# Two feed-forward stages of a hybrid transformer on Trainium2: weight splits issued earlier in the first, squares summed in two halves and a held first product in the second

## The chip, the cores and the metric

The kernel runs on one core of one Trainium2 chip, as one program. The metric is the device time of one execution in microseconds; lower is better. The core's engines work at the same time, each through its own instruction stream in a fixed order: TensorE (PE, matmuls; its weight loads are listed as PEld), VectorE (DVE), ScalarE (ACT), GpSimd (POOL). SyncE (SP) issues the DMAs.

## The reference

Two layers over 512 latent tokens and 256 context tokens of width 1024, in float32. Layer 0 mixes by grouped attention, layer 1 by a gated recurrence (HGRN2) in both directions; each is followed by a gated feed-forward (SwiGLU, hidden width 2816). Norms are modulated by vectors made from a condition `c`. Cut to what matters here:

```python
h = h + gt1_l * y_l                      # y_l: attention or recurrence, after its output product w_o
h = h + gt2_l * swiglu(modulate(rms_norm(h, norm_ffn_w[i]), sh2_l, sc2_l), ffn_w_in[i], ffn_w_out[i])

def rms_norm(x, w):                      # sum of squares over the 1024 features of a token
    return x * lax.rsqrt(jnp.mean(x * x, axis=-1, keepdims=True) + NORM_EPS) * w

def swiglu(h, w_in, w_out):
    a, u = jnp.split(h @ w_in, 2, axis=-1)
    return (jax.nn.silu(a) * u) @ w_out
```

The first feed-forward (layer 0) works on 768 tokens (latent and context), the second on 512.

## The kernel before

Activations are kept transposed: `hT[o]` holds 128 features (row o of 8) by all tokens. Every float32 product is made as three matmuls of a faster format (`mm3`, lines 114 to 118): each operand is split into a high part and a low part, hi x hi, hi x lo, lo x hi. `split` makes them: the high part is a cast on ACT (L88), the low part a subtraction on DVE or POOL (L93). Weights arrive by DMA in a ring of four raw buffers, `load_next` (L922) queues the next one on SP when an older buffer has been split.

A feed-forward (`ffn`) takes the hidden width in 22 units of 128 columns, each with two weight blocks, `("w", j, 0)` for a and `("w", j, 1)` for u. In the text w01 is block 1 of unit 0, and so on. The first units (two in layer 0, four in layer 1) are computed plainly: `plain_split` splits a unit's weights, `plain` multiplies them with the tokens in two halves of H columns, `plain_hidden` makes silu(a) * u and splits it into `gh` and `gl`. All later units use Strassen's scheme (Winograd's form) of seven products per unit, `m1` to `m7`, on the four quarters b11, b12, b21, b22 of the normalised input `x`. It needs sums of weight quarters, made on POOL in place in the raw buffers (`sums`, L1147 to L1150, and `sum4`, L1155), and differences of input quarters (t1 to t4). Each weight operand is one entry of a list of units, split in list order by `split_next`. The first entry's quarter a11 is overwritten by `sums`, so `sums` follows its split; the second entry, a12, is followed by `sum4`.

The start of each feed-forward overlaps with the end of the mixer before it:

- Layer 0, `start_attention`: the plain units run while POOL and DVE form the differences (L1294 and L1298 on POOL, L1301 and L1305 on DVE). Behind the last differences come two calls of `split_next`. Then PE goes on with `m1`, `m2`, `m5` (its bank is y), `m6` (operand t2), `m4` (bank w, operand t4).
- Layer 1, `start_recurrence`: `hgrn_wo_last` yields the recurrence's output rows in two halves of 256 tokens, eight rows each. A row is a few matmuls into a bank `hwo` and a residual addition on DVE (L687). Rows 6 and 7 of a half share a bank. For each row ACT squares it (L275, the first directly into the accumulator, L271) and POOL adds the square to `acc_n` (L276). Then `rstd_cols` sums over the features with matmuls against ones (`ssq`, L282), DVE and POOL make the reciprocal root (`rc`, L289 and L291), `rstd_psum` spreads it over partitions (DVE L297, PE L301), and `xhalf` makes the normalised and modulated operand of one row: DVE L960, ACT L962, cast L88, low part L93. Then come the first products (`ffi`).

A planner orders each engine's instructions before the kernel runs. It starts from program order and moves an instruction ahead when its own model of the times says that it is ready earlier. `pin` ties an instruction behind the one that the program issues just before it on the same engine. In `split`, `late="h"` pins the cast and `late="l"` the subtraction.

Of the kernel before, what the change touches and what calls it, by code (L numbers as in the profile page):

```python
# [8 lines left out]
F32 = mybir.dt.float32  # L9
# [7 lines left out]
P = 128  # L17
D = 1024
KT = D // P
# [28 lines left out]
def kernel(  # L48
# [10 lines left out]
    PE, DVE, ACT, POOL = nc.tensor, nc.vector, nc.scalar, nc.gpsimd  # L59
# [20 lines left out]
    def bank(name):  # L80
        return psums["pool"].tile([P, 512], F32, tag="b", bufs=psums["bufs"]["b"], name=name)
# [29 lines left out]
        split(hi, lo, raw, eng, hi_eng)  # L111
        return hi, lo

    def mm3(ps, ahi, alo, bhi, blo, first, last, onto=False):
        kw = dict(skip_group_check=True) if onto else {}
        PE.matmul(ps, ahi, bhi, start=first, stop=False, **kw)  # L116
        PE.matmul(ps, ahi, blo, start=False, stop=False, **kw)  # L117
        PE.matmul(ps, alo, bhi, start=False, stop=last, **kw)  # L118

    pin = tc.keep_in_program_order  # L120
# [34 lines left out]
    ones = cst.tile([P, P], F32, name="ones")  # L155
# [119 lines left out]
            ACT.activation(sq, h, AF.Square)  # L275
            (eng or DVE).tensor_tensor(acc, acc, sq, op=ALU.add)  # L276

    def rstd_cols(pl, acc, n, tag="rc", late=False):
        nt = n // P
        pc = bank("ssq")  # L280
        for t in range(nt):
            m = PE.matmul(pc[:, 2 * t : 2 * t + 2], acc[:, t * P : (t + 1) * P], ones[:, 0:2], start=True, stop=True)  # L282
            if late:
                pin(m)
        return rstd_of(pl, pc, nt, tag)

    def rstd_of(pl, pc, nt, tag="rc"):
# [586 lines left out]
    def ffn(layer, only_lat, pre, begin, tail=None):  # L874
        n = NL if only_lat else T
        H = n // 2
# [24 lines left out]
        def ctile(tag, bufs):  # L901
            return fp.tile([P, H], F32, tag=tag, bufs=bufs, name=tag)
# [40 lines left out]
        def plain_split(j, i, late=""):  # L943
            if j > 1 or i == 0 and (j == 0 or not layer):
                t = ring_tile()
            else:
                slot, p_ = {(0, 1): (3, fp), (1, 0): (1, fp), (1, 1): (2, fp if layer else hnp)}[j, i]
                t = [p_.tile([P, 4 * H], F32R, tag=f"xt{slot}{c}", name=f"w{j}1{c}")[:, 0:1024] for c in "hl"]
            pool_ = (j, i) == (0, 0) or j > 1 and i if layer else j == 0
            split(t[0], t[1], raws.pop(("w", j, i)), POOL if pool_ else DVE, late=late)  # L950
            w0[j, i] = t

# [10 lines left out]
            xh, xl = xops[("b1" if k < 4 else "b2") + "12"[h]]  # L963
            split(xh[:, k % 4], xl[:, k % 4], x[k][:, a0:e0], DVE if k % 2 else POOL)

        def plain(ps, j, i, k, h, first, last):
            hi, lo = w0[j, i]
            xh, xl = xops[("b1" if k < 4 else "b2") + "12"[h]]
            c = slice(k * P, (k + 1) * P)
            if h not in ps:  # L970
                ps[h] = xbank("ffi")[:, 0:H]
            mm3(ps[h], hi[:, c], lo[:, c], xh[:, k % 4], xl[:, k % 4], first, last)

        gh, gl = {}, {}

# [6 lines left out]
        def plain_hidden(j, h, psa, psu):  # L982
            c = ctile("c22", 2)
            ACT.activation(c, psa[h], AF.Silu)
            DVE.tensor_tensor(c, psu[h], c, op=ALU.mult)
            split(gh[j][:, h * H : h * H + H], gl[j][:, h * H : h * H + H], c)
# [254 lines left out]
        def start_attention():  # L1241
# [54 lines left out]
            for i in range(4):  # L1296
                b11, b12, b21, b22 = blocks(i)
                pin(POOL.tensor_tensor(b12, b22, b12, op=ALU.subtract))  # L1298
            for i in range(4):
                b11, b12, b21, b22 = blocks(i)  # L1300
                pin(DVE.scalar_tensor_tensor(b22, b11, -1.0, b22, op0=ALU.mult, op1=ALU.subtract))  # L1301
            plain_hidden(0, 1, *ps0)
            for i in range(4):
                b11, b12, b21, b22 = blocks(i)
                pin(DVE.scalar_tensor_tensor(b21, b22, -1.0, b21, op0=ALU.mult, op1=ALU.subtract))  # L1305
            split_next()
            split_next()
            xops["t3"] = operand("t3")
            for i in range(4):
                xsplit("t3", i, x[i][:, H:n])  # L1310
# [9 lines left out]
        def start_recurrence():  # L1320
# [4 lines left out]

            def products(j, h, i, ks):
                for k in ks:
                    plain(ps[j][i], j, i, k, h, k == 0, k == KT - 1)

            for h in range(2):  # L1330
                hs = slice(h * H, (h + 1) * H)
                for i in range(KT):
                    o = next(pre)
                    sumsq_add(acc_n[:, hs], fp, hT[o][:, hs], o, i == 0, POOL, tag="sw", bufs=2, width=512)
                    if h == 0 and i == 0:
                        plain_split(0, 0, "l")
                    if h == 0 and i == KT - 1:
                        plain_split(0, 1, "l")
                    if h == 1 and i == 1:
                        plain_split(1, 0, "l")  # L1340
                    if h == 1 and i == 2:
                        rst[0] = rstd_psum(ctile("c22", 2), rc[0], H)
                    if h == 1 and i >= 4:
                        xhalf(i - 4, 0)
                rc[h] = rstd_cols(fp, acc_n[:, hs], H, f"rc{h}")
            for _ in pre:
                pass
            for _ in range(2):
# [1 line left out]
            for k in range(KT):  # L1350
                if k >= 4:
                    xhalf(k, 0)
                for i in range(2):
                    products(0, 0, i, [k])
            plain_split(1, 1, "l")
            rst[1] = rstd_psum(ctile("c22", 2), rc[1], H)
            for k in order[:2]:
                xhalf(k, 1)
# [8 lines left out]
            for i_, k in enumerate(order):  # L1367
                for i in range(2):
                    plain(ps[0][i], 0, i, k, 1, i_ == 0, i_ == KT - 1)
            plain_split(2, 0)  # L1370
            plain_split(2, 1, "l")
            for _ in range(2):
                load_next()
# [374 lines left out]
    def hgrn_wo_last():  # L1748
        ks = (GH - 2, GH - 1)
        wo = []  # L1750
        for k in ks:
            t = [ring.tile([P, 1024], F32R, tag=tag, bufs=3, name=f"{tag}_hwo{k}") for tag in ("whi", "wlo")]
            split(t[0], t[1], hv.pop(("w", k)))
            wo.append(t)
        banks = []

        def first_rows(h):
            oh, ol = hv["o", GH - 2]
            a, e = h * (NL // 2), (h + 1) * (NL // 2)
            for o in range(6):  # L1760
                osl = slice(o * P, (o + 1) * P)
                if h == 0:
                    banks.append(xbank("hwo"))
                mm3(banks[o][:, a:e], wo[0][0][:, osl], wo[0][1][:, osl], oh[:, a:e], ol[:, a:e], True, False, True)

        first_rows(0)
        yield None
        os_ = [hv.pop(("o", k)) for k in ks]
        for h, (_, a, e) in enumerate(SPH):
            both = bank("hwo") if h == 0 else None  # L1770
            for o in range(KT):
                osl = slice(o * P, (o + 1) * P)
                if o < 6:
                    ps, todo = banks[o][:, a:e], (1,) if h == 0 else (0, 1)
                else:
                    both = both or xbank("hwo")
                    ps, todo = both[:, (o - 6) * 256 : (o - 6) * 256 + 256], (0, 1)
                for i in todo:
                    mm3(ps, wo[i][0][:, osl], wo[i][1][:, osl], os_[i][0][:, a:e], os_[i][1][:, a:e],
                        i == 0, i == 1, True)  # L1780
                residual(o, ps, 1, 2, 0, a, e)
                yield o

# [116 lines left out]
```

## Time and profile before

| | |
|---|---|
| runs | 1820.36, 1823.32, 1823.44 us; median 1823.32 |
| profiled execution | 1821.68 us, span of its instructions 1819.9 us |
| granted TensorE clock, mean | 0.99 |
| matmuls | 11749, PE busy 1755.3 us |
| first feed-forward's start | about 455 to 505 us of the span |
| second feed-forward's start | about 1437 to 1515 us of the span |
| HBM read | 162.36 MB, 90 GB/s |

Times in rows are microseconds from the span's start, and a row of one engine in order of time begins with its start and its length; neighbours of the same form are merged (xN), and square brackets give idle time of the engine before the row and what ended it. A waits row reads: who waited, for whom, microseconds in total, times, the longest. A windows row gives each engine's busy microseconds, with the number of instructions, in one stretch. Matmuls are pipelined: one may start before the last has ended, so the pace is read from starts or from counts.

### The profile page before, as it was taken

How to read it: one execution, taken by the hardware profiler on the slowest of the kernel's cores; microseconds unless marked ns; L12 is line 12 of the kernel's file. 1: busy time of each engine (PE TensorE's matmuls, PEld its weight loads, DVE VectorE, ACT ScalarE, POOL GpSimd, SP SyncE). 2: the span in 40 equal slices, each digit the busy share in tenths (PEclk: the TensorE clock that was granted, in tenths of full speed). 3: DMA queues.
4: the chain of work that ended last, by engine and by line, in shares of the span. 5: the costliest groups of instructions: out<-in, count | busy, mean ns of one | idle time of the engine just before them, and what ended most of it. 6: DMA issues, size and time to landing. Idle time of an engine off the chain costs nothing.

```text
span 1819.9 us, 30696 instructions
## 1 busy us (share of the span) xinstructions
PE 1755.3 (96%) x11749; PEld 1606.9 (88%) x11749; DVE 1300.5 (71%) x2291; ACT 867.2 (48%) x1768; POOL 637.7 (35%) x583
## 2 busy tenths in 40 slices
PE   8988999999999999999999999999999899999998
PEld 6778678988899999999998999899898799999997
DVE  4587588888888878787865555665747758786764
ACT  4342787676642424333354443343434445554545
POOL 1244254345522304131414333144325544443420
PEclk9999999999999999999999999999999999999999
DMA  8533520002124243445331211222211223333322
GB/s 319 176 105 84 163 79 24 1 24 64 30 87 129 73 137 93 146 133 153 108 116 34 70 59 59 70 82 70 81 56 38 67 59 112 101 106 106 99 60 83
DMA packets 213459, 166.45 MB, mean 91 GB/s; under 512 B 7952, under 2 KB 190400, under 8 KB 213312
## 3 DMA queue, kind: packets, MB, share of 16 engines
q1 hardware_dynamic: 213024, 163.43, 29.2%
q8 instruction: 93, 1.52, 0.4%
q10 hardware_dynamic: 288, 1.05, 0.1%
q14 instruction: 54, 0.44, 0.1%
HBM read 162.36 MB, written 2.10 MB: 90 GB/s over the span
## 4 chain that ended last, share of the span: by engine, by line
PE 78%; DVE 9%; POOL 4%; ACT 4%; issue 2%; DMA 2%; SPq 0%; POOLq 0%; DVEq 0%; ACTq 0%
PE ffo L118 5%; PE ffo L116 5%; PE ffo L117 5%; PE x L116 4%; PE x L117 4%; PE x L118 4%; PE pt L714 3%; PE y L118 2%; PE y L116 2%; PE y L117 2%; PE lv L1643 2%; PE hz L116 2%; PE hz L117 2%; PE hz L118 2%; PE sc L656 2%
## 5 line engine op out<-in xcount | busy, mean ns | idle before, releaser
L1650 POOL TENSOR_TENSOR KD<-KD,tot 128x384 f32<-128x384 f32 x96 | 102.6, 1092 | 82.1 <-ACT kc L1633 78.4
L704 POOL TENSOR_SCALAR pf<-pf,st 128x768 f32<-128x768 f32 (+1 forms) x96 | 73.6, 769 | 128.1 <-DVE st L703 91.6
L687 DVE SCALAR_TENSOR_TENSOR hT<-ffo,modc,hT 128x512 f32<-128x512 f32 (+1 forms) x122 | 78.7, 649 | 48.2 <-PE ffo L118 48.2
L118 PE MATMUL ffo<-gh,wlo_w 128*128 128x512 f32 (+1 forms) x304 | 102.9, 339 | 0.0
L117 PE MATMUL ffo<-gl,whi_w 128*128 128x512 f32 (+1 forms) x304 | 102.4, 337 | 0.0
L116 PE MATMUL ffo<-gh,whi_w 128*128 128x512 f32 (+1 forms) x304 | 102.0, 338 | 0.0
L239 DVE SCALAR_TENSOR_TENSOR adacc<-adw,csil,adacc 128x512 f32<-128x512 f32 x98 | 84.5, 871 | 7.5 <-DMA adw<-in_ada_w_dram 7.4
L93 DVE TENSOR_TENSOR ptl<-pt,pth 128x384 fp32r<-128x384 f32 (+1 forms) x160 | 79.9, 524 | 12.4 <-ACT pth L88 11.2
L88 ACT CAST pth<-pt 128x384 fp32r<-128x384 f32 (+1 forms) x160 | 69.9, 461 | 34.3 <-PE pt L714 22.6
L700 DVE TENSOR_REDUCE st<-sc 128x1 f32<-128x768 f32 (+1 forms) x96 | 74.2, 773 | 15.3 <-PE sc L657 12.6
L702 ACT ACTIVATE pf<-sc,st 128x768 f32<-128x768 f32 (+1 forms) x96 | 73.4, 765 | 19.3 <-DVE st L700 18.4
L1650 DVE TENSOR_TENSOR QD<-QD,tot 128x256 f32<-128x256 f32 x96 | 52.0, 582 | 41.2 <-PE lv L1643 41.1
L1633 ACT COPY kc<-KD 128x256 f32<-128x256 f32 x112 | 43.4, 414 | 75.8 <-PE lv L1643 43.8
L714 PE MATMUL pt<-ident,pf 128*128 128x128 f32 x448 | 72.2, 275 | 5.2 <-DVE ptl L93 3.9
L116 PE MATMUL ffo<-gh,foh 128*128 128x512 f32 (+1 forms) x186 | 71.4, 384 | 0.0
L118 PE MATMUL ffo<-gh,fol 128*128 128x512 f32 (+1 forms) x186 | 70.8, 381 | 0.2 <-DVE fol L93 0.2
L117 PE MATMUL ffo<-gl,foh 128*128 128x512 f32 (+1 forms) x186 | 70.9, 381 | 0.0
L1709 POOL TENSOR_SCALAR oss<-oss 128x4 f32<-128x4 f32 (+1 forms) x9 | 4.7, 524 | 181.8 <-DVE oss L1708 181.7
L1643 PE MATMUL lv<-QD,kc 128*128 128x128 f32 x448 | 63.4, 286 | 4.5 <-DVE QD L1650 2.4
L1643 PEld LDWEIGHTS lv<-QD,kc 128*128 128x128 f32 x448 | 58.7, 192 | 8.8 <-ACT kc L1633 3.8
L714 PEld LDWEIGHTS pt<-ident,pf 128*128 128x128 f32 x448 | 51.2, 140 | 14.4 <-issue 6.4
L117 PEld LDWEIGHTS ffo<-gl,whi_w 128*128 128x128 f32 x304 | 57.4, 189 | 6.9
(1101 smaller groups left out, 6793.9 us busy)
## 6 DMA issues: line engine op xcount, KB each, us to landing
adw<-in_ada_w_dram SPq DMA_DIRECT2D x40, 512.0 KB, 4.7
adw<-in_ada_w_dram SPq DMA_DIRECT2D x80, 256.0 KB, 2.9
raw_hz<-in_hgrn_w_in_dram SPq DMA_DIRECT2D x14, 512.0 KB, 3.8
adr<-in_ada_w_dram SPq DMA_DIRECT2D x16, 256.0 KB, 4.7
adr<-in_ada_w_dram SPq DMA_DIRECT2D x8, 512.0 KB, 7.5
raw_wq<-in_attn_w_qkv_dram SPq DMA_DIRECT2D x8, 512.0 KB, 5.7
raw_wo<-in_attn_w_o_dram SPq DMA_DIRECT2D x8, 512.0 KB, 3.5
raw_hv<-in_hgrn_w_in_dram SPq DMA_DIRECT2D x8, 512.0 KB, 4.9
```

What stands on the lines that cost most here:

```text
L93: m = (eng or DVE).tensor_tensor(lo, src, hi.bitcast(F32), op=ALU.subtract)
L116: PE.matmul(ps, ahi, bhi, start=first, stop=False, **kw)
L117: PE.matmul(ps, ahi, blo, start=False, stop=False, **kw)
L118: PE.matmul(ps, alo, bhi, start=False, stop=last, **kw)
L239: pin(DVE.scalar_tensor_tensor(a, raw, cc, a, op0=ALU.mult, op1=ALU.add))
L687: DVE.scalar_tensor_tensor(hT[o][:, a:e], ps, mcol(layer, ch, o, v), hT[o][:, a:e], op0=ALU.mult, op1=ALU.add)
L700: DVE.tensor_reduce(st3[:, 0:1], ps[:, :nk], op=ALU.max, axis=AX.X, negate=True)
L702: ACT.activation(pf, ps[:, :nk], AF.Exp, bias=st3[:, 0:1], accum_out=st3[:, 1:2])
L704: POOL.tensor_scalar(pf, pf, st3[:, 2:3], 1.0, op0=ALU.mult, op1=ALU.mult)
L714: PE.transpose(pt[:, i * P : (i + 1) * P], pf[:, (i0 + i) * P : (i0 + i + 1) * P], ident)
L1643: PE.matmul(ps[:, cs], kc[:, cs], mv, start=True, stop=True)
L1650: eng.tensor_tensor(view, view, f, op=ALU.mult)
```

## The change

In the first feed-forward the two `split_next` calls move: the first stands ahead of the differences L1301, the second ahead of L1305.

In the second feed-forward:

- The squares go into two accumulators: even rows by POOL into `acc_n`, odd rows by DVE into the tile of `x[7]`, which is not in use yet. `rstd_cols` sums both with the matmuls (two for each token block instead of one).
- The second half's `rstd_cols` moves behind the products of unit 0's first half and the split of w11.
- The low parts of w01 and w11 move from DVE to POOL. w01 and w10 are split at earlier rows; w10's cast is pinned too, and w20's low part is pinned.
- The very first product (unit 0, block 0, first half, k = 0) is pinned behind the last of the recurrence's output products.
- In `hgrn_wo_last` the matmuls of rows 6 and 7 are issued together, ahead of row 6's residual.

```diff
-    def mm3(ps, ahi, alo, bhi, blo, first, last, onto=False):
+    def mm3(ps, ahi, alo, bhi, blo, first, last, onto=False, hold=False):
         kw = dict(skip_group_check=True) if onto else {}
-        PE.matmul(ps, ahi, bhi, start=first, stop=False, **kw)
+        m = PE.matmul(ps, ahi, bhi, start=first, stop=False, **kw)
+        if hold:
+            pin(m)
...
-    def rstd_cols(pl, acc, n, tag="rc", late=False):
+    def rstd_cols(pl, accs, n, tag="rc", late=False):
         nt = n // P
         pc = bank("ssq")
+        accs = accs if isinstance(accs, list) else [accs]
         for t in range(nt):
-            m = PE.matmul(pc[:, 2 * t : 2 * t + 2], acc[:, t * P : (t + 1) * P], ones[:, 0:2], start=True, stop=True)
-            if late:
-                pin(m)
+            for i, acc in enumerate(accs):
+                m = PE.matmul(pc[:, 2 * t : 2 * t + 2], acc[:, t * P : (t + 1) * P], ones[:, 0:2],
+                              start=i == 0, stop=i == len(accs) - 1)
+                if late:
+                    pin(m)
...
-            pool_ = (j, i) == (0, 0) or j > 1 and i if layer else j == 0
+            pool_ = j == 0 or i if layer else j == 0
...
-        def plain(ps, j, i, k, h, first, last):
+        def plain(ps, j, i, k, h, first, last, hold=False):
...
-            mm3(ps[h], hi[:, c], lo[:, c], xh[:, k % 4], xl[:, k % 4], first, last)
+            mm3(ps[h], hi[:, c], lo[:, c], xh[:, k % 4], xl[:, k % 4], first, last, hold=first and hold)
...
                 pin(POOL.tensor_tensor(b12, b22, b12, op=ALU.subtract))
+            split_next()
             for i in range(4):
                 b11, b12, b21, b22 = blocks(i)
                 pin(DVE.scalar_tensor_tensor(b22, b11, -1.0, b22, op0=ALU.mult, op1=ALU.subtract))
+            split_next()
             plain_hidden(0, 1, *ps0)
             for i in range(4):
                 b11, b12, b21, b22 = blocks(i)
                 pin(DVE.scalar_tensor_tensor(b21, b22, -1.0, b21, op0=ALU.mult, op1=ALU.subtract))
-            split_next()
-            split_next()
...
-                    plain(ps[j][i], j, i, k, h, k == 0, k == KT - 1)
+                    plain(ps[j][i], j, i, k, h, k == 0, k == KT - 1, j == h == i == 0)
+
+            last = KT - 1
+            x[last] = gslot(10 + last, F32, f"x{last}")
+
+            def halfsums(h):
+                return [acc_n[:, h * H : h * H + H], x[last][:, h * H : h * H + H]]
...
-                    sumsq_add(acc_n[:, hs], fp, hT[o][:, hs], o, i == 0, POOL, tag="sw", bufs=2, width=512)
-                    if h == 0 and i == 0:
-                        plain_split(0, 0, "l")
-                    if h == 0 and i == KT - 1:
-                        plain_split(0, 1, "l")
-                    if h == 1 and i == 1:
-                        plain_split(1, 0, "l")
+                    if i % 2:
+                        sumsq_add(halfsums(h)[1], fp, hT[o][:, hs], o, i == 1, DVE, tag=("c11", "c12")[i // 2 % 2],
+                                  bufs=1, width=H)
+                    else:
+                        sumsq_add(halfsums(h)[0], fp, hT[o][:, hs], o, i == 0, POOL, tag="sw", bufs=2, width=512)
+                    if h == 0 and i < 2:
+                        plain_split(0, i, "l")
+                    if h == 1 and i == 0:
+                        plain_split(1, 0, "hl")
...
-                rc[h] = rstd_cols(fp, acc_n[:, hs], H, f"rc{h}")
+                if h == 0:
+                    rc[h] = rstd_cols(fp, halfsums(h), H, f"rc{h}")
...
             plain_split(1, 1, "l")
+            rc[1] = rstd_cols(fp, halfsums(1), H, "rc1")
             rst[1] = rstd_psum(ctile("c22", 2), rc[1], H)
...
-            plain_split(2, 0)
+            plain_split(2, 0, "l")
...
-                    ps, todo = banks[o][:, a:e], (1,) if h == 0 else (0, 1)
+                    ps, todo = banks[o][:, a:e], [(o, (1,) if h == 0 else (0, 1))]
                 else:
                     both = both or xbank("hwo")
-                    ps, todo = both[:, (o - 6) * 256 : (o - 6) * 256 + 256], (0, 1)
-                for i in todo:
-                    mm3(ps, wo[i][0][:, osl], wo[i][1][:, osl], os_[i][0][:, a:e], os_[i][1][:, a:e],
-                        i == 0, i == 1, True)
+                    ps, todo = both[:, (o - 6) * 256 : (o - 6) * 256 + 256], [(6, (0, 1)), (7, (0, 1))][: 2 * (7 - o)]
+                for o_, parts in todo:
+                    osl = slice(o_ * P, (o_ + 1) * P)
+                    pr_ = ps if o_ < 6 else both[:, (o_ - 6) * 256 : (o_ - 6) * 256 + 256]
+                    for i in parts:
+                        mm3(pr_, wo[i][0][:, osl], wo[i][1][:, osl], os_[i][0][:, a:e], os_[i][1][:, a:e],
+                            i == 0, i == 1, True)
                 residual(o, ps, 1, 2, 0, a, e)
```

More of the change, by code (lines that the diff above doesn't have):

```diff
@@ L1771, in hgrn_wo_last @@
             for o in range(KT):
-                osl = slice(o * P, (o + 1) * P)
                 if o < 6:
-                    ps, todo = banks[o][:, a:e], (1,) if h == 0 else (0, 1)
+                    ps, todo = banks[o][:, a:e], [(o, (1,) if h == 0 else (0, 1))]
                 else:
                     both = both or xbank("hwo")
-                    ps, todo = both[:, (o - 6) * 256 : (o - 6) * 256 + 256], (0, 1)
-                for i in todo:
-                    mm3(ps, wo[i][0][:, osl], wo[i][1][:, osl], os_[i][0][:, a:e], os_[i][1][:, a:e],
-                        i == 0, i == 1, True)
+                    ps, todo = both[:, (o - 6) * 256 : (o - 6) * 256 + 256], [(6, (0, 1)), (7, (0, 1))][: 2 * (7 - o)]
[5 more added lines that the diff above has]
+                            i == 0, i == 1, True)
                 residual(o, ps, 1, 2, 0, a, e)
```

## The prediction

> **What bounds the kernel now.** I read the page's busy table first, then PE's waits, then windows around the two places that the diff touches, then single engines in order of time.
>
> ```profile
> PE 1755.3 (96%) x11749; PEld 1606.9 (88%) x11749; DVE 1300.5 (71%) x2291; ACT 867.2 (48%) x1768; POOL 637.7 (35%) x583
> PE y L118 <- DVE wlo_w L93: 2.3, 1, 2.3
> PE x L116 <- ACT xt2h L88: 0.8, 1, 0.8
> PE ssq L282 <- POOL acc_n L276: 3.2, 1, 3.2
> PE ffi L116 <- ACT xw L88: 1.8, 1, 1.8
> ```
>
> TensorE is busy 96% of the span, so only places where it starves, or runs at a reduced clock, can give time back. The diff touches two: 485 to 500 us (first feed-forward, place A) and 1440 to 1465 us (second, place B). Windows there, each with one of the same length in which PE never starves:
>
> ```profile
> 485.00:500.00 15.00, 11.37 (x46) 9.86 (x45) 10.04 (x20) 8.68 (x19) 6.79 (x5) 0.77 0.16 44
> 500.00:515.00 15.00, 15.00 (x88) 15.00 (x88) 13.42 (x19) 7.67 (x17) 6.45 (x4) 1.00 0.28 85
> 1440.00:1465.00 25.00, 18.78 (x134) 17.68 (x133) 17.37 (x35) 17.26 (x40) 16.39 (x20) 0.86 0.29 86
> 1475.00:1500.00 25.00, 25.00 (x211) 25.00 (x211) 12.28 (x25) 8.30 (x21) 10.25 (x11) 1.00 0.16 48
> ```
>
> Columns: window, its length, busy us (instructions) of PE, PEld, DVE, ACT and POOL, then granted clock, DMA share and GB/s. At A 46 matmuls take 15 us; at the undisturbed rate they take 46 x 15/88 = 7.8, so A loses 7.2 us. At B 134 x 25/211 = 15.9, so B loses 9.1 us. Together 16.3 us (0.9%) is the most that the change can give. PE is full behind both places (second and fourth row), so what is won there reaches the end.
>
> **A: the split ahead of the differences.** What PE waits for, from POOL, ACT and DVE in order of time:
>
> ```profile
> 473.23 5.22 POOL L1298 TENSOR_TENSOR x<-x,x 128x384 f32<-128x384 f32 x4
> 484.23 2.61 POOL L1147 TENSOR_TENSOR raw_('w', 2, 0)_5658<-raw_('w', 2, 0)_5658,raw_('w', 2, 1)_5660 128x512 f32<-128x512 f32 x1 [5.78 <-DVE wlo_w L93]
> 486.92 1.29 POOL L1147 TENSOR_TENSOR raw_('w', 2, 1)_5660<-raw_('w', 2, 1)_5660 128x512 f32<-128x512 f32 x1
> 488.25 0.62 ACT L88 CAST whi_w<-raw_('w', 2, 1)_5660 128x512 fp32r<-128x512 f32 x1 [5.83 <-POOL raw_('w', 2, 1)_5660 L1147]
> 476.20 1.37 DVE L1301 SCALAR_TENSOR_TENSOR x<-x,x 128x384 f32<-128x384 f32 x1
> 477.50 1.37 DVE L1301 SCALAR_TENSOR_TENSOR x<-x,x 128x384 f32<-128x384 f32 x1
> 481.60 1.95 DVE L1305 SCALAR_TENSOR_TENSOR x<-x 128x384 f32<-128x384 f32 x4
> 483.47 1.28 DVE L93 TENSOR_TENSOR wlo_w<-raw_('w', 2, 0)_5658,whi_w 128x512 fp32r<-128x512 f32 x2
> 490.54 0.66 DVE L93 TENSOR_TENSOR gl<-c,gh 128x384 fp32r<-128x384 f32 x1 [4.38 <-ACT gh L88]
> 491.12 0.68 DVE L93 TENSOR_TENSOR wlo_w<-raw_('w', 2, 1)_5660,whi_w 128x512 fp32r<-128x512 f32 x1
> ```
>
> POOL's weight sums overwrite a block whose low half DVE must have split. That split stands behind eight differences, so POOL idles 5.78 us; ACT's queue waits on the sums, gh and gl stand behind, and DVE idles 4.38 us before unit 2's low half (491.12), for which PE waits. From there DVE runs almost without a gap until PE has its next operands, so A's gain is the shift of that row.
>
> The change lets the first split run at about 476.2 and POOL's sums from 478.45, the end of L1298: 5.8 us earlier. Nothing is added, no DMA moves (units 0 and 1 release no raw buffer). What is queued behind the moved splits are the differences (0.64 us each split, 1.28/2), which feed t2 and t4, and these are split only behind row 491.12. But the sums now fall into a stretch where DVE is full. At 476.20 and 477.50 the differences start 1.30 us apart beside POOL; alone they start 0.49 apart (1.95/4). So a POOL instruction costs a DVE instruction about 0.8 us. Four sums: 3.3 us. Ends: no slowing, gain 4.4; slowing by the sums' whole length (1.29 each, 5.2), loss 0.8. The L1301 rows are the same pair of engines, some microseconds earlier in the same queues, so I take them: 4.4 - 3.3, **A = -1.1 us**. That is far under A's 7.2 because DVE, not PE, then sets A.
>
> [...]
>
> **B: two sums of squares, first product held.** The chain before the first product:
>
> ```profile
> 1439.67 0.75 POOL acc_n L276
> 1441.32 1.78 POOL acc_n L276
> 1443.17 1.59 POOL acc_n L276
> 1441.28 1.22 DVE L93 TENSOR_TENSOR w11l<-raw_('w', 1, 0)_14914,w11h 128x1024 fp32r<-128x1024 f32 x1
> 1442.80 1.37 DVE L93 TENSOR_TENSOR w01l<-raw_('w', 0, 1)_14912,w01h 128x1024 fp32r<-128x1024 f32 x1
> 1435.05 2.39 POOL L93 TENSOR_TENSOR wlo_w<-raw_('w', 0, 0)_14910,whi_w 128x1024 fp32r<-128x1024 f32 x1
> 1436.98 1.04 ACT L88 CAST w01h<-raw_('w', 0, 1)_14912 128x1024 fp32r<-128x1024 f32 x1
> 1447.26 0.61 PE L282 MATMUL ssq<-ones,acc_n 128*128 128x2 f32 x4 [3.23 <-POOL acc_n L276]
> 1447.90 0.16 DVE L289 TENSOR_SCALAR rc<-ssq 128x2 f32<-128x2 f32 x1 [3.73 <-PE ssq L282]
> 1449.36 1.22 PE L301 MATMUL rstd<-c,ones 128*128 128x128 f32 x4 [0.34 <-DVE c L297]
> 1452.35 0.58 PE L116 MATMUL ffi<-xw,whi_w 128*128 128x256 f32 x1 [1.77 <-ACT xw L88]
> 1452.94 0.41 PE L116 MATMUL hwo<-oth,whi_hwo 128*128 128x256 f32 x1
> 1437.52 3.84 DVE L687 SCALAR_TENSOR_TENSOR hT<-hwo,modc,hT 128x256 f32<-128x256 f32 x9
> 1448.00:1456.00 8.00, 2.47 (x6) 0.57 0.02 6
> 1450.00:1455.00 5.00, 3.23 (x15) 2.93 (x15) 3.85 (x11) 4.20 (x12) 4.25 (x6) 0.50 0.01 2
> ```
>
> Seven POOL adds in a row, two of them stretched from 0.75 to 1.78 and 1.59 beside DVE's splits, end at 1447.26. PE waits 3.23 us with output products still to do (the hwo row at 1452.94), and 1.77 more for the first operand. Step by step:
>
> Adds: POOL keeps three of seven, but first takes the split of w01 (ACT's cast ends 1438.02, plus 2.39: 1440.4). Three adds of 0.75 to 1.1 end at 1442.7 to 1443.7. DVE's three of the other sum come behind residuals that end about 1441.4 (1437.52 + 3.84), so not later; its splits w01 and w11 (second unit), 1.2 to 1.4 each, leave for POOL, which pays 2.39 for each. I take 1443.7 because DVE's remaining split still competes: **-3.5**. Ends: 1440.4 + 3 x 1.78 = 1445.7 (-1.5), 1442.7 (-4.5).
>
> ssq: eight matmuls for four, at 0.61 for four: between 0 and +0.6, I take **+0.4**, on the path.
>
> Squares: the window with one engine is ACT's second-half squares, six in 2.47 us amid the casts that feed the first products. With PE's output products no longer stopped they fall ahead of the casts: 0 to -2.5, **-1.0**.
>
> Clock: 0.50 from 1450 to 1455, with PE busy 3.23 us; at full clock this is 1.6 us of work, and the neighbours add some: 0 to -2, **-1.0**.
>
> ```profile
> 1460.67 1.21 DVE L93 TENSOR_TENSOR w11l<-raw_('w', 1, 1)_14916,w11h 128x1024 fp32r<-128x1024 f32 x1
> 1463.24 1.26 DVE L960 SCALAR_TENSOR_TENSOR x<-hT,a_ffn,rstd 128x256 f32<-128x256 f32 x3 [0.22 <-PE rstd L301]
> 1468.36 0.28 PE L116 MATMUL ffi<-xb12h,whi_w 128*128 128x256 f32 x1
> 1457.05 0.51 PE L282 MATMUL ssq<-ones,acc_n 128*128 128x2 f32 x4
> 1461.81 1.21 DVE L93 TENSOR_TENSOR wlo_w<-raw_('w', 2, 0)_15107,whi_w 128x1024 fp32r<-128x1024 f32 x1
> 1479.78 0.28 PE L116 MATMUL ffi<-xw,whi_w 128*128 128x256 f32 x1
> ```
>
> The rest has one answer each. The hold is an order on PE, not a wait on another engine: the first product goes behind work that PE has ready, and behind it queue only the other first products. What ran early before (1452.35, two products) is 0.8 us. Rows 6 and 7 share a bank; issued together, row 7's products no longer wait for row 6's residual, while that residual waits for 6 products more, 0.7 us, under DVE's other residuals (1437.52). w11's cast for the first half is pinned behind a square, and w20's split (1461.81) behind the second half's operands, 18 us ahead of its first product (1479.78). The second half's ssq (1457.05) moves behind the first products; its chain now ends (1463.24) 5.1 us before its own products (1468.36), and that is the cover. POOL's split of w11 for the second half of the unit (formerly DVE's, 1460.67) has 24 products as cover, 24 x 25/211 = 2.8 us against 2.39. The split of w01 ends earlier, so its raw buffer and SP's next load come earlier; no load is added. **B = -3.5 + 0.4 - 1.0 - 1.0 = -5.1 us.**
>
> Sum: -6.2 us. The profiled execution took 1821.68 (span 1819.9), 1.6 below the median of the runs, 1823.32; so 1815.5 against its own time, and **1817.1** as a median.
>
> **The rivals.** *Lock at A:* sums and DVE exclude one another entirely: A = +0.8, B as above, 1823.3 - 4.3 = 1819.0. For it: the 1.30 us starts; against it: the add at 1441.32 was stretched by 1.0 beside a split of 1.22, not by all of it. Chance 0.13.
>
> *Both places recover:* if POOL's sums slip between DVE's reads and the remaining gaps are too short to halve the clock, A gives 4.4, and B the ends of its terms, -4.5 + 0.4 - 2.5 - 2.0 = -8.6: 1823.3 - 13.0 = 1810.3. For it: at both places more is lost (7.2 and 9.1); against it: DVE is full at A. [...] Chance 0.13.
>
> *Order eats B:* each engine's order is fixed beforehand, so ssq may be placed earlier and PE may wait there as long, with output products behind it. B then keeps 1.5 or so, total -2.6, 1820.7: no measurable change. The same holds if the scheduled order hardly moves. For it: DVE waited 3.73 us for ssq with residuals to do. Chance 0.18.
>
> *Slower:* the second half's ssq lands on PE behind all 48 products of the next unit pair (5.7 us) instead of inside the first ones (1457.05). Then the whole chain from ssq to first product, 1452.35 - 1447.26 = 5.1 us, lies open and about 2 us of half clock follow; and if its power on POOL stands in front of w11's split, that comes later by the 2.1 us from ssq to rstd (1447.26 to 1449.36): -6.2 + 9.2 = +3.0, 1826.3. It decides from the point where ssq starts less than 5.1 us before PE runs out of products. Against it: ssq is ready early and unpinned. Chance 0.08.
>
> **How the numbers follow.** My forecast has 0.48 (own range 1814 to 1819.5). Measurement tells 0.2%, 3.6 us, from no change. Faster: 0.48 + 0.13 + most of the lock case's 0.13, less the forecast's weak tail: 0.70. Slower by over 0.2%: the slow case with A's worst: 0.06. The rest 0.24. The range 1810 to 1823 takes in all but the slow case.
>
> **What would show it.** A: POOL's L1147 starts near 478.5, DVE's 4.38 us gap before gl is gone, but its splits and differences stretch; wlo_w for y lands about 1.1 us earlier. B: ssq starts near 1443.7, no wait of 3.2 us, all hwo products before the first ffi, first ffi near 1448.5, clock above 0.86 in that window. Wrong if ssq still waits over 2 us, if the second rstd has PE waiting, or if time moves anywhere outside A and B.

## The result and the profile after

The change made the kernel slower: 1827.79 us median (1824.58 to 1829.5) against 1822.16 (1820.24 to 1823.44), ratio 1.0029, 95% interval 1.0018 to 1.0041, about 5.3 us. The forecast was 1817.1, faster by 6.2 us than the 1823.32 of three earlier runs of the kernel before.

In the new kernel's line numbers the adds are L278 (before L276), the ssq matmuls L286, rc L294, c L302, rstd L306, the three products L116, L119 and L120, the squares L273 and L277, the modulation L967. The page's busy row and PE's waits after:

```profile
PE 1758.6 (96%) x11757; PEld 1610.6 (88%) x11757; DVE 1306.8 (72%) x2295; ACT 865.0 (47%) x1768; POOL 636.5 (35%) x577
PE y L120 <- DVE wlo_w L93: 3.4, 1, 3.4
PE ffi L116 <- ACT xw L88: 2.5, 1, 2.5
PE ssq L286 <- POOL acc_n L278: 2.4, 1, 2.4
PE ffi L119 <- DVE xw L93: 2.3, 1, 2.3
```

The wait for y grew from 2.3 to 3.4 us. At place B two waits, 3.2 and 1.8 us, became three: 2.4, 2.5 and 2.3. The windows of the prediction, and place B in pieces of 5 us:

```profile
485.00:500.00 15.00, 10.76 (x44) 9.64 (x43) 13.62 (x27) 9.34 (x22) 1.28 (x2) 0.77 0.14 43
1440.00:1465.00 25.00, 19.47 (x109) 18.76 (x107) 14.80 (x32) 14.73 (x34) 10.97 (x14) 0.73 0.21 61
1440.00:1445.00 5.00, 2.56 (x21) 2.35 (x20) 3.06 (x8) 3.23 (x9) 2.61 (x4) 0.98 0.69 196
1445.00:1450.00 5.00, 5.00 (x25) 5.00 (x25) 2.71 (x5) 1.24 (x4) 2.04 (x2) 0.50 0.00 0
1450.00:1455.00 5.00, 2.64 (x16) 2.43 (x15) 3.24 (x9) 3.26 (x7) 0.73 (x1) 0.84 0.36 107
1455.00:1460.00 5.00, 4.89 (x22) 4.80 (x23) 3.78 (x10) 5.00 (x16) 2.99 (x4) 0.50 0.00 0
```

PE is busier at B than before (19.47 us, before 18.78) and does less: 109 matmuls for 134, at 0.73 of the clock for 0.86. The clock halves twice, to 0.50 from 1445 to 1450 and from 1455 to 1460. Busy time alone would have hidden this; the count and the clock beside it tell it.

The chain of work that ended last names a cause that no part of the diff touches. Its columns are start, length, what:

```profile
1437.58 4.69 DMA raw_('fo', 0, 0)_15563<-in_ffn_w_out_dram
1442.71 0.42 ACT sq L277
1443.26 0.73 POOL acc_n L278
1444.04 0.39 PE ssq L286 x2
```

The single instructions around it, from ACT, PE, DVE and POOL in order of time:

```profile
1442.29 0.51 ACT L88 CAST foh<-raw_('fo', 0, 0)_15563 128x384 fp32r<-128x384 f32 x1 [1.77 <-DMA raw_('fo', 0, 0)_15563<-in_ffn_w_out_dram]
1446.38 0.42 PE L286 MATMUL ssq<-ones,x 128*128 128x2 f32 x2
1447.69 0.16 DVE L294 TENSOR_SCALAR rc<-ssq 128x2 f32<-128x2 f32 x1 [2.29 <-PE ssq L286]
1451.74 1.05 ACT L88 CAST whi_w<-raw_('w', 2, 0)_15100 128x1024 fp32r<-128x1024 f32 x1 [2.98 <-PE hwo L119]
1453.01 1.03 ACT L88 CAST whi_w<-raw_('w', 2, 1)_15102 128x1024 fp32r<-128x1024 f32 x1
1453.95 0.51 ACT L967 ACTIVATE x<-x,modc 128x256 f32<-128x256 f32 x1
1455.11 0.58 PE L116 MATMUL ffi<-xw,whi_w 128*128 128x256 f32 x1 [2.47 <-ACT xw L88]
1462.16 0.16 DVE L294 TENSOR_SCALAR rc<-ssq 128x2 f32<-128x2 f32 x1 [3.38 <-PE ssq L286]
1463.77 2.53 POOL L93 TENSOR_TENSOR w11l<-raw_('w', 1, 1)_14916,w11h 128x1024 fp32r<-128x1024 f32 x1
1464.02 2.90 DVE L93 TENSOR_TENSOR xw<-x,xw 128x256 fp32r<-128x256 f32 x2
```

The cast of the first output weights (foh, for the output products of this feed-forward) now stands ahead of the squares of rows 6 and 7 on ACT, and ACT waits 1.77 us for its DMA. In the trace before it stood between the squares of these two rows, and its data was there:

```profile
1445.11 0.50 ACT L88 CAST foh<-raw_('fo', 0, 0)_15563 128x384 fp32r<-128x384 f32 x1
```

The first sum is complete nearly when the prediction said (ssq starts at 1444.04, forecast 1443.7), but the other sum's ssq starts at 1446.38, with output products at half clock (0.50) between, and rc comes at 1447.69, where it was before (1447.90). Then it takes 4.1 us to the first rstd, before 1.5. On DVE the split of w11 stands ahead of c, and on PE rstd stands behind the output products, which run at half clock:

```profile
1448.16 1.22 DVE L93 TENSOR_TENSOR w11l<-raw_('w', 1, 0)_14914,w11h 128x1024 fp32r<-128x1024 f32 x1
1449.29 0.95 DVE L302 TENSOR_TENSOR c<-ident,rc 128x256 f32<-128x256 f32 x1
1451.79 0.61 PE L306 MATMUL rstd<-c,ones 128*128 128x128 f32 x4
```

Next, ACT casts w20 and w21 ahead of the first operand, though their first product comes at 1485.12. Later DVE waits 3.38 us for the second half's ssq with the last low parts of the first half's operands queued behind, and then runs them beside POOL's split of w11 (1463.77); PE waits 2.3 us for one of them.

### The profile page after: what moved, and what is told of

Same layout as the page of the kernel before. It is cut to its first block, busy times and chain, and to the rows that moved or that the text cites. A ratio compares the mean times of both kernels' runs of the same rounds, so it can differ in the third digit from the quotient of the medians.

```text
span 1825.9 us, 30697 instructions
## 1 busy us (share of the span) xinstructions
PE 1758.6 (96%) x11757; PEld 1610.6 (88%) x11757; DVE 1306.8 (72%) x2295; ACT 865.0 (47%) x1768; POOL 636.5 (35%) x577
## 4 chain that ended last, share of the span: by engine, by line
PE 80%; DVE 10%; ACT 4%; POOL 3%; issue 2%; DMA 1%; SPq 0%; POOLq 0%; DVEq 0%; ACTq 0%
PE ffo L120 5%; PE ffo L116 5%; PE ffo L119 5%; PE x L116 4%; PE x L119 4%; PE x L120 4%; PE pt L719 3%; PE y L120 2%; PE y L116 2%; PE y L119 2%; PE lv L1658 2%; PE hz L116 2%; PE hz L119 2%; PE hz L120 2%; PE sc L661 2%
## 5 line engine op out<-in xcount | busy, mean ns | idle before, releaser
L120 PE MATMUL ffo<-gh,wlo_w 128*128 128x512 f32 (+1 forms) x304 | 103.1, 339 | 0.0
L119 PE MATMUL ffo<-gl,whi_w 128*128 128x512 f32 (+1 forms) x304 | 102.6, 337 | 0.0
L116 PE MATMUL ffo<-gh,whi_w 128*128 128x512 f32 (+1 forms) x304 | 102.3, 339 | 0.0
L93 DVE TENSOR_TENSOR ptl<-pt,pth 128x384 fp32r<-128x384 f32 (+1 forms) x160 | 79.8, 523 | 12.4 <-ACT pth L88 11.2
L705 DVE TENSOR_REDUCE st<-sc 128x1 f32<-128x768 f32 (+1 forms) x96 | 74.1, 772 | 13.9 <-PE sc L662 11.1
L707 ACT ACTIVATE pf<-sc,st 128x768 f32<-128x768 f32 (+1 forms) x96 | 73.3, 764 | 19.2 <-DVE st L705 18.3
L116 PE MATMUL ffo<-gh,foh 128*128 128x512 f32 (+1 forms) x186 | 71.5, 384 | 0.0
L120 PE MATMUL ffo<-gh,fol 128*128 128x512 f32 (+1 forms) x186 | 71.0, 382 | 0.2 <-DVE fol L93 0.2
L119 PE MATMUL ffo<-gl,foh 128*128 128x512 f32 (+1 forms) x186 | 71.0, 382 | 0.0
L119 PEld LDWEIGHTS ffo<-gl,whi_w 128*128 128x128 f32 x304 | 57.6, 190 | 6.9
```

Of the source, the lines that this page charges most:

```text
L93: m = (eng or DVE).tensor_tensor(lo, src, hi.bitcast(F32), op=ALU.subtract)
L116: m = PE.matmul(ps, ahi, bhi, start=first, stop=False, **kw)
L705: DVE.tensor_reduce(st3[:, 0:1], ps[:, :nk], op=ALU.max, axis=AX.X, negate=True)
L707: ACT.activation(pf, ps[:, :nk], AF.Exp, bias=st3[:, 0:1], accum_out=st3[:, 1:2])
```

## The experiments

Place B is measured in each trace from the last row of otl on DVE (the low half of the recurrence's last output operand, 1437.12 before) to the start of the first ssq, of the first product, and of the first product of the second half, in us. "This" is the median. The kernel before was run anew beside each group, so differences in the text are taken from the ratios: 0.0010 is 1.8 us.

| kernel | this, us | ratio to before, 95% | ssq | first product | second half |
|---|---|---|---|---|---|
| before | | | 10.1 | 15.2 | 31.2 |
| the change | 1827.8 | 1.0029 (1.0018 to 1.0041) | 7.2 | 18.3 | 36.8 |
| a_only | 1821.4 | 1.0005 (0.9996 to 1.0013) | 10.1 | 15.9 | 32.3 |
| two_sums | 1818.2 | 0.9987 (0.9978 to 0.9996) | 5.9 | 12.5 | 29.5 |
| splits | 1826.4 | 1.0027 (1.0016 to 1.0039) | 11.7 | 19.5 | 36.3 |
| hold67 | 1825.2 | 1.0024 (1.0015 to 1.0033) | 10.2 | 21.8 | 35.5 |
| after_nosplits | 1820.7 | 1.0001 (0.9992 to 1.0009) | 5.9 | 13.9 | 28.9 |
| two_rows67 | 1819.6 | 0.9996 (0.9987 to 1.0005) | 5.9 | 13.9 | 29.5 |
| after_fopin | 1824.5 | 1.0016 (1.0007 to 1.0024) | 6.0 | 14.2 | 33.1 |
| after_w2 | 1823.5 | 1.0011 (1.0002 to 1.0020) | 6.9 | 17.0 | 33.0 |
| after_fopin_w2 | 1821.6 | 1.0006 (0.9997 to 1.0015) | 6.0 | 13.5 | 30.6 |
| two_fopin_w2 | 1816.9 | 0.9981 (0.9969 to 0.9992) | 5.9 | 12.5 | 28.2 |
| before_fopin_w2 | 1821.2 | 0.9999 (0.9991 to 1.0008) | 10.1 | 15.2 | 31.2 |
| splits_fopin_w2 | 1822.7 | 1.0009 (0.9999 to 1.0019) | 11.3 | 18.3 | 33.7 |
| two_rows67_pins | 1816.9 | 0.9970 (0.9958 to 0.9982) | 5.9 | 12.4 | 26.2 |
| best_again (same program) | 1817.2 | 0.9976 (0.9967 to 0.9985) | 5.9 | 12.4 | 27.3 |
| two_splits_pins | 1820.7 | 1.0001 (0.9992 to 1.0010) | 6.0 | 15.5 | 31.4 |
| after_norows_pins | 1821.9 | 1.0002 (0.9994 to 1.0011) | 6.0 | 15.9 | 31.6 |
| pins_engines | 1818.7 | 0.9989 (0.9980 to 0.9998) | 5.9 | 15.0 | 28.8 |
| pins_places | 1820.1 | 0.9992 (0.9983 to 1.0000) | 6.2 | 13.5 | 28.5 |

### The parts, one at a time

Each starts from the kernel before. a_only has the two `split_next()` moved up in `start_attention` and nothing else; hold67 has the held first product and rows 6 and 7 issued together, as in the change's diff. two_sums has the new `rstd_cols`, `halfsums(h)` for both halves where rc was made before, and

```diff
-    sumsq_add(acc_n[:, hs], fp, hT[o][:, hs], o, i == 0, POOL, ...)
+    if i % 2:
+        sumsq_add(halfsums(h)[1], fp, hT[o][:, hs], o, i == 1, DVE, ...)
+    else:
+        sumsq_add(halfsums(h)[0], fp, hT[o][:, hs], o, i == 0, POOL, ...)
```

splits has the five edits on the plain splits:

```diff
-    pool_ = (j, i) == (0, 0) or j > 1 and i if layer else j == 0
+    pool_ = j == 0 or i if layer else j == 0
...
-                    if h == 0 and i == 0:
-                        plain_split(0, 0, "l")
-                    if h == 0 and i == KT - 1:
-                        plain_split(0, 1, "l")
-                    if h == 1 and i == 1:
-                        plain_split(1, 0, "l")
+                    if h == 0 and i < 2:
+                        plain_split(0, i, "l")
+                    if h == 1 and i == 0:
+                        plain_split(1, 0, "hl")
...
-            plain_split(2, 0)
+            plain_split(2, 0, "l")
```

> The kernel before with the first feed-forward's two splits moved, and nothing of the second. The traces of before and after put the loss at the second stage: between the last recurrence output rows and the 288th first product PE falls 5.5 us behind, while around 485 to 500 us it only loses 0.3. Theory order (the second stage's fixed instruction order costs the time): here 0 to +0.6 us, 1822 to 1823, and PE waits about 3.4 us for the low half of y as in the changed kernel. Rival (the POOL sums beside DVE cost more than the trace showed, and the second stage only inherits it): +2 us or more.

> The kernel before with the squares in two accumulators alone: the splits stay where they were, no product is held, rows 6 and 7 are issued as before, the second half's sum stays ahead of the first products. Theory order: the two sums are themselves the loss, because the eight ssq matmuls do not stand together: one, then 15 output products, then three, then 7 more products, then rstd. The first ssq starts near 1444 instead of 1447.3, yet the reciprocal root is no earlier than before; +1 to +4 us. Rival splits (the moved weight splits and casts are the loss, the two sums help as forecast): -2 to -4 us.

> The kernel before with the weight splits of the second stage alone: low parts of w01 and w11 on POOL, earlier places, w10's cast and w20's low part pinned; one sum of squares, no hold. Theory order: the sum of squares still ends POOL's chain, now behind w01's 2.4 us, so ssq about 1 to 2 us later, and DVE is freed of 2.4 us: between -1 and +2 us. Rival splits: this alone gives most of the loss, +3 to +6 us, with ACT's casts of w20 and w21 ahead of the first operand.

> The kernel before with the first product held and rows 6 and 7 issued together, one sum of squares as before. PE's order then has ssq after 59 output products, 15 more, rstd, the last 4, the second half's ssq, then all products. Theory order: PE does its output products while it waits and is not interrupted: -0.5 to -2 us. Rival (the hold itself costs, because the first products wait for the last output rows and the second ssq stands in front of them): +1 to +3 us.

A moved alone cost nothing that can be measured. Two sums alone gain 2.4 us: the order theory, by which two sums lose by themselves, fell. Splits alone (4.9 us) and hold with rows 6 and 7 alone (4.4 us) each lose nearly as much as the whole change; the losses don't add. In the trace of splits, on ACT and POOL:

```profile
1443.89 0.51 ACT L88 CAST foh<-raw_('fo', 0, 0)_15563 128x384 fp32r<-128x384 f32 x1 [3.09 <-DMA raw_('fo', 0, 0)_15563<-in_ffn_w_out_dram]
1441.26 2.40 POOL L93 TENSOR_TENSOR w01l<-raw_('w', 0, 1)_14912,w01h 128x1024 fp32r<-128x1024 f32 x1
```

This is the same DMA wait, longer, with squares behind it, and POOL's split stands in the middle of the adds. In hold67, PE:

```profile
1457.29 1.01 PE L284 MATMUL ssq<-ones,acc_n 128*128 128x2 f32 x4 [4.85 <-POOL acc_n L278]
1458.16 0.56 PE L116 MATMUL ffi<-xw,whi_w 128*128 128x256 f32 x1
```

With the first product tied behind the output products, the second half's ssq was ordered ahead of all 48 first products, and PE waits 4.85 us for it. In the change, where rc[1] is issued later, this doesn't happen; there the hold alters nothing: without it the planned orders of PE, DVE, ACT and POOL are the same.

### Undoing the splits, adding the rows, pinning four casts

after_fopin_w2 is the change with four of ACT's casts pinned:

```diff
-            split(g[0], g[1], u["src"](), late="l" if begun[0] else "")
+            fo0 = layer and u["done"] in (("fo", 0, 0), ("fo", 0, 1))
+            split(g[0], g[1], u["src"](), late="hl" if fo0 else "l" if begun[0] else "")
...
             for k in order[2:]:
                 xhalf(k, 1)
+            plain_split(2, 0, "hl")
+            plain_split(2, 1, "hl")
             plain_hidden(1, 0, *ps[1])
...
-            plain_split(2, 0, "l")
-            plain_split(2, 1, "l")
```

after_nosplits is the change with the diff of splits undone, two_rows67 is two_sums with rows 6 and 7 issued together, and two_fopin_w2 is two_sums with the pins above.

> The changed kernel, whole, with four casts of ScalarE pinned: the two of the output weights (foh, units 0 and 1) behind the recurrence's start, and the two of the third unit's weights (w20, w21) behind the second half's operands. TensorE's scheduled order in the disputed region stays that of the changed kernel. Cast theory: ScalarE's waiting 1.77 us for the DMA of foh ahead of two squares and its 2.1 us of w20 and w21 ahead of the first operand are what lost the time, so the last add comes about 1.3 earlier, the first product 2 to 3 earlier, and with it the second stretch of half clock goes: 1822 to 1824, level with before to +2. Order theory (ssq and rstd stand behind 11 and 20 output-product matmuls that run at half clock): nothing comes of it, 1826 to 1828.

> The changed kernel with the five edits on the splits undone (engine of w11, places and pins as in the kernel before); two sums, held first product, rows 6 and 7 together, later rc[1] and part A stay. Since the splits alone cost 4.9 us, the split theory says that this gives them back: 1821 to 1823. Order theory: the scheduled order of TensorE still has rstd behind all output products (22 of them after ssq, against 7 in two_sums) and the casts of w20 and w21 still stand ahead of the first operand, so most of the loss stays: 1824 to 1827.

> Two sums of squares, and rows 6 and 7 issued together, and nothing else of the change. TensorE's scheduled order becomes 50 output-product matmuls, ssq, 6, ssq x3, 22, rstd (two_sums alone: 50, ssq, 15, ssq x3, 7, rstd), and w20's and w21's casts come to stand ahead of the first operand. Rows theory: the order that this edit brings is what spoils two sums, 1822 to 1824.5 against 1818.2 for two sums alone. Prediction's view (the edit costs nothing, under DVE's other residuals): 1817.5 to 1819.

> Two sums of squares alone of the change, with the same four casts pinned late. Cast theory: foh and w20 (1.05) no longer stand between squares and operands, so 0.5 to 2 us under two sums alone: 1816 to 1818. If casts do not matter: 1818.2, as two sums alone.

PE's order in after_fopin_w2 is that of the change up to the second half's first ssq (behind it some first products change places), and 4 of the 5.3 us are gone: most of the loss came from what stood where on ACT. Undoing the splits alone also takes 5 back: with them as before, the planner puts foh's casts behind the first half's squares. The ratio of two_rows67 lies 0.0009 over that of two_sums, each just at the edge of the other's interval, so that rows 6 and 7 cost something there is neither shown nor ruled out.

### Which casts, and a control

after_fopin is the change with the first hunk of the pins (foh) alone, after_w2 with the second (w20, w21) alone; before_fopin_w2 and splits_fopin_w2 have both hunks on the kernel before and on splits.

> The changed kernel with only the two casts of the output weights (foh) pinned late; w20's and w21's casts stay ahead of the first operand. In the changed kernel ScalarE waited 1.77 us on foh's DMA, and the last add of the first half ended 1.3 us late for it, after which the clock halved. If the foh wait is the start of the loss: most of it comes back, 1822 to 1824. If the casts of w20 and w21 are: 1826 to 1827.5.

> The counterpart: the changed kernel with only w20's and w21's casts pinned behind the second half's operands; foh's casts stay ahead of two squares. If the foh wait is the start of the loss: ssq still starts near 1444 and the output products behind it still run at half clock; only the 1.0 us by which the first ready operand waited comes back, 1825.5 to 1827. If w20 and w21 are: 1822 to 1824.

> The kernel before with the same four casts pinned late and nothing of the change: control for two_fopin_w2 (ratio 0.9981). There the foh casts stood between two groups of squares (1445.11) and w20's behind the operands already. If the pins alone bring that gain: 1817 to 1818.5. If it is the two sums: 1819.5 to 1821, level with before.

> The kernel before with the splits' five edits (which alone cost 4.9 us) and the four casts pinned late. If the edits lose by what they let the planner put ahead of the squares on ScalarE (foh, waiting 3.09 us on its DMA): level with before to +1.5, 1820 to 1822. If they lose by POOL's split of w01 amid the adds, or by w11's cast ahead of the squares: 1824 to 1826.

Each pair gives back part: 2.4 us (foh) and 3.3 us (w20, w21), both together 4.2. By the expectations after_w2 speaks for w20 and w21 as the cause, but after_fopin fits neither reading: both pairs cost time, and the parts overlap. How the foh pair acts is read from PE's first wait and the window behind it, first after_fopin, then after_w2:

```profile
1443.99 0.38 PE L286 MATMUL ssq<-ones,acc_n 128*128 128x2 f32 x2 [1.23 <-POOL acc_n L278]
1445.00:1450.00 5.00, 4.77 (x39) 4.36 (x37) 3.90 (x8) 2.15 (x5) 2.04 (x2) 1.00 0.13 37
```

```profile
1442.04 0.38 PE L286 MATMUL ssq<-ones,acc_n 128*128 128x2 f32 x2 [2.17 <-POOL acc_n L278]
1445.00:1450.00 5.00, 5.00 (x24) 5.00 (x25) 3.29 (x6) 0.84 (x2) 2.76 (x3) 0.50 0.35 104
```

Without the DMA wait PE idles 1.23 us and the output products behind run at full clock (39 matmuls in the 5 us); with it 2.17 us, and they run at half (24 in a full 5 us). The pins alone, on the kernel before, change nothing: the gain of two_fopin_w2 is that of two sums. On splits they take back 3.3 of the 4.9 us.

### What is left of the loss

All have both hunks of the pins. two_rows67_pins adds them to two_rows67, and best_again is the same program once more; two_splits_pins has two sums and the diff of splits; after_norows_pins is the change with rows 6 and 7 as before. pins_engines is two_rows67_pins with the line `pool_ =` of splits, pins_places with the rest of that diff.

> Two sums of squares, rows 6 and 7 issued together, and the four casts pinned late. TensorE's order: 50 output products, ssq, 6, ssq x3, 22, rstd, first products (two_fopin_w2: 50, ssq, 15, ssq x3, 7, rstd). If rows 6 and 7 are what is left of the loss: 3 to 4.5 us over two_fopin_w2, level with before, 1820 to 1822. If the splits are: within 1 us of two_fopin_w2 and 2.5 to 3.5 under before, 1817.5 to 1819.

> Two sums of squares, the splits' five edits, and the four casts pinned late. If the splits are what is left: POOL's 2.4 us split of w01 stands ahead of its first add and ssq starts about 1442.8 instead of 1440.5, so 2 to 4 us over two_fopin_w2, 1820 to 1822. If rows 6 and 7 are: 1817.5 to 1819.

> The whole change with the four casts pinned late and rows 6 and 7 issued as before. The held first product now counts (six output products ahead of it) and the second half's ssq stands behind 20 first products in one piece. If rows 6 and 7 are what is left of the loss: 2.5 to 4 us under before, 1817.5 to 1819. If the splits are: 1821 to 1823, as after_fopin_w2 (1.1 over before).

> Two sums of squares, rows 6 and 7 together, four casts pinned late, and of the splits only the change of engine: w01's and the second block of w11's low halves on POOL (2.4 and 2.57 us there, 1.21 on DVE), places and pins as in the kernel before. Engine theory: DVE's low parts of the first operands stand still beside POOL's split of w11 as in after_fopin_w2 (0.41 us became 2.60 at 1459.23, PE waited 0.8), 2 to 4 us over best_again. Place theory: within 1 us of it.

> Two sums of squares, rows 6 and 7 together, four casts pinned late, and of the splits only the places and pins (w01's right behind the second square, w11's first block behind the second half's first square with its cast pinned), engines as in the kernel before. Place theory: the cast of w11's second block now stands ahead of the squares and that of its first between those of the second half, DVE's split of w01 ahead of its adds: 2 to 4 us over best_again. Engine theory: within 1 us of it.

> The same kernel as two_rows67_pins (ratio 0.9970, 1816.9): two sums of squares, rows 6 and 7 issued together, four casts pinned late. Expected 1816 to 1818.5, 3 to 5 us under before.

With the pins rows 6 and 7 are innocent: the program that has them (two_rows67_pins, and again best_again) has the lowest ratio of all, and the change without them stays level with before. That program beats the kernel before by 4.4 to 5.5 us, and the change by about 10. With the casts held late, the splits cost 3.6 us on two_fopin_w2; on best_again their engine part costs 2.4 and their places 2.9. The engine part shows its mechanism. DVE and POOL in pins_engines, then the same add of DVE in two_rows67_pins:

```profile
1445.24 2.57 DVE L276 TENSOR_TENSOR x<-x,sq 128x256 f32<-128x256 f32 x1
1445.16 2.36 POOL L93 TENSOR_TENSOR w01l<-raw_('w', 0, 1)_14912,w01h 128x1024 fp32r<-128x1024 f32 x1
1447.86 0.38 PE L284 MATMUL ssq<-ones,x 128*128 128x2 f32 x2 [1.40 <-DVE x L276]
```

```profile
1443.12 0.41 DVE L276 TENSOR_TENSOR x<-x,sq 128x256 f32<-128x256 f32 x1
```

DVE's last add takes 2.57 us instead of 0.41: it begins 0.08 us after the start of POOL's split and ends 0.29 us after the split's end, and PE waits 1.40 us for it. That is what moving w01's split to POOL brought here. In the change w01's split runs earlier (1437.80) and meets residuals, which are as fast as with POOL idle (six in 2.43 us; in two_rows67_pins, with POOL idle, 2.44); there it is the split of w11 that meets DVE's low parts (1463.77 and 1464.02), two of which take 2.90 us, where one took 0.41 at 1458.37. How the places act wasn't taken further apart; in pins_places PE waits 0.99 us at rstd for c, in two_rows67_pins not at all.

## Why the prediction was wrong

**A, -1.1 forecast.** The path was right, the price too small. POOL's sums start at 477.89 (forecast 478.45), and DVE's idle 4.38 us before gl shrank to 0.58, so the move worked as described; then the price ate it. On POOL and DVE of the changed kernel:

```profile
479.56 1.49 POOL L1152 TENSOR_TENSOR raw_('w', 2, 1)_5660<-raw_('w', 2, 1)_5660 128x512 f32<-128x512 f32 x1
476.98 6.06 DVE L1307 SCALAR_TENSOR_TENSOR x<-x,x 128x384 f32<-128x384 f32 x4
490.76 0.68 DVE L93 TENSOR_TENSOR wlo_w<-raw_('w', 2, 1)_5660,whi_w 128x512 fp32r<-128x512 f32 x1
```

Four differences take 6.06 us, 1.5 apart where the prediction took 1.30 (and 0.49 for them alone), and the sum takes 1.49 for 1.29. wlo_w comes at 490.76 (491.12 before) in a trace that was 0.65 us ahead: A lost 0.3 there. The runs of a_only allow -0.7 to +2.4, which takes in the lock rival's +0.8 and not the forecast. (The prediction's four times 0.8 is 3.2, not 3.3; nothing hangs on it.)

**B, -5.1 forecast, +5.5 in the traces.** From otl to the second half's first product it took 31.2 us before and 36.8 in the change. Step by step, change against before: to the first ssq -2.9, from there to rc +3.0, to rstd +2.6, to the first product +0.3, to the second half's first product +2.5. The sum had no term for the third step, and for the last only part of the clock's.

**Adds, -3.5.** Right where it was aimed, -2.9 in the change: ssq starts 7.2 us after otl (before 10.1), and 5.9 in two_sums. In the change POOL's last add waits 1.29 us for the square behind foh.

**ssq, +0.4.** Mis-sized. Counted was the time of four more matmuls, not what is ordered between the pairs. From the first ssq to rc it took 0.64 us before and 3.65 in the change. rc comes 10.9 us after otl in the change, 10.8 before: all that the adds won was given back here. In two_sums, at full clock (1.00 from 1440 to 1445), rc comes after 8.8.

**Squares, -1.0.** No gain came: from rstd to the first product it took 3.3 us, before 3.0. The casts of w20 and w21 came in front of the first operand instead.

**Clock, -1.0.** Wrong sign: 0.73 for 0.86 over the 25 us. The wait for ssq shrank only to 2.44 us, still over the 2 us that the prediction named as a sign of being wrong, and behind it the clock halved (0.50 from 1445 to 1450) under the output products that were meant to run early; rstd stood behind them (+2.6).

**"The rest has one answer each."** This is the step that failed most. The edits on the splits were priced by their own durations and given cover; alone they cost 4.9 us. Two things were missing. An edit shifts what the planner takes to be ready, and instructions that are not pinned (foh, w20, w21) change place on an engine that the edit doesn't touch. And a split on POOL wasn't only 2.4 us of POOL: beside it a DVE add took 2.57 us instead of 0.41 (pins_engines), which the 1.30 us rows at A (0.49 alone) had shown in small. The second half's chain wasn't covered either: its rc stood in DVE's queue ahead of low parts that PE needed first, and PE waited 2.3 us for one of them. The hold did cost nothing in the change, but only because rc[1] was issued later.

**Rivals.** Order eats B (0.18) had the mechanism, ssq with output products around it and no gain left, and fell 7 us short (1820.7 for 1827.8), since it left out ACT's order and the lower clock (0.73 at B). The slower rival (0.08) had the sign, and its side condition came true: the second half's power on POOL stood in front of w11's split. Its mechanism, rstd of the second half laid open behind the products, isn't what PE waited for: it waited for a low part queued behind that rc on DVE and beside POOL's split (1464.02). Of "both places recover" (0.13) nothing came: neither place gained. That short gaps leave the clock alone was its assumption: in the runs waits of about 1.5 and of 2.26 us were followed by 1.00 and by a lower clock (0.77, 0.66).

## What to carry to other kernels

Where a planner orders the engines, price an edit by the order that it leaves on every engine, not by the instructions that it moves: a cast whose result is needed late can come to stand, unpinned, in front of an urgent square and wait there for a DMA (1.77 us in the change, 3.09 in splits). Pin what isn't urgent before moving what is. And read matmul counts and clock beside busy time: PE busy 5.00 us of 5 at half clock is a loss (25 matmuls from 1445 to 1450 in the change; 211 in 25 us, or 42 in 5, where the clock was 1.00).

## What the runs showed of the hardware

A DVE add that began 0.08 us after the start of a POOL split ended 0.29 us after the split's end: 0.41 us became 2.57 beside POOL's 2.36 (pins_engines). DVE's residuals ran on: six in 2.43 us beside the split of w01 in the change, and 2.44 with POOL idle (two_rows67_pins, from 1437.65). What sets the two cases apart was not shown. DVE and POOL in the change:

```profile
1437.22 2.43 DVE L692 SCALAR_TENSOR_TENSOR hT<-hwo,modc,hT 128x256 f32<-128x256 f32 x6
1437.80 2.41 POOL L93 TENSOR_TENSOR w01l<-raw_('w', 0, 1)_14912,w01h 128x1024 fp32r<-128x1024 f32 x1 [0.67 <-ACT w01h L88]
```

The lock rival took the like of POOL's sums at A, and its +0.8 lies in a_only's interval (-0.7 to +2.4).

The clock halved behind some of PE's waits and not behind others. Waits of 2.17 us (after_w2) and 2.44 us (the change) were followed by 0.50, one of 1.23 us (after_fopin) by 1.00. A wait of 2.26 us did both: in the change, before a product at 1466.63, the clock stayed at 1.00; in after_fopin, before the same kind of product at 1462.59, it fell (0.66 from 1462 to 1467). The windows, the change first, then after_fopin:

```profile
1465.00:1470.00 5.00, 3.37 (x28) 3.37 (x29) 2.50 (x4) 0.46 (x2) 1.30 (x1) 1.00 0.36 105
```

```profile
1462.00:1467.00 5.00, 4.41 (x24) 4.41 (x25) 1.12 (x3) 0.38 (x1) 0.26 (x1) 0.66 0.37 105
```

Near 1.5 us the same program does both. The first operand's wait and the windows around it, two_rows67_pins first, then best_again:

```profile
1449.61 0.39 PE L116 MATMUL ffi<-xw,whi_w 128*128 128x256 f32 x1 [1.55 <-ACT xw L88]
1450.00:1455.00 5.00, 4.64 (x37) 4.24 (x37) 3.76 (x12) 4.03 (x11) 2.57 (x4) 1.00 0.05 15
```

```profile
PE ffi L116 <- ACT xw L88: 1.6, 1, 1.6
1445.00:1450.00 5.00, 3.44 (x18) 3.23 (x19) 4.65 (x12) 4.70 (x13) 3.10 (x4) 0.77 0.33 96
```

Place B took 26.2 us in the one and 27.3 in the other, so a single trace of this kernel is uncertain by about 1 us there; the clock is the difference that the two traces show (1.00 from 1440 to 1465 in the one, 0.93 in the other).
